# A hybrid encoder on one Trainium2 core: the attention's hand-written step order is replaced by another

## Chip, cores and metric

The kernel runs on one core of one Trainium2 chip. The metric is device microseconds of one execution, as the median of several. The engines are called by the profile's names: PE (TensorE; PEld its weight loads), ACT (ScalarE), DVE (VectorE), POOL (GpSimd) and SP, which here only issues DMAs.

## The reference, cut to what matters

Two layers on x of shape 256 x 1024, float32. Each layer is a half SwiGLU, a mixer and a half SwiGLU; the second layer's mixer is multi-head latent attention, and the change lies in it alone:

```python
cq = rmsnorm(h @ w_dq, q_norm_g)                     # 256 wide
q = (cq @ w_uq).reshape(B, L, 16, 64 + 32)           # rotary part turned with cos, sin
ckv_full = h @ w_dkv                                 # 128 + 32 wide
kv = (rmsnorm(ckv_full[..., :128], kv_norm_g) @ w_ukv).reshape(B, L, 16, 64 + 64)
s = einsum('bqhd,bkhd->bhqk', qn, k_nope) + einsum('bqhr,bkr->bhqk', qr, k_rope)
p = softmax(s * scale); o = einsum('bhqk,bkhd->bqhd', p, v)
x = x + o @ w_o
```

## The kernel before, in words

Every float32 operand of a product is split into a high part (rounded by ACT, `split_hi`, L180) and a low residue (source minus high part, `split_lo`, L184, on DVE or, where a flag says so, on POOL). A product is then three matmuls (`mm3`, L199 to L201): high by high, high by low, low by high. PE runs these triples nearly all the time.

The attention (`mla`, L915) treats 16 heads as 8 pairs p, the two heads of a pair as e = 0, 1, and 256 tokens as two tiles t. Weights come as ten units, each one 1 MB or smaller DMA into one of two `raw` buffers and then split into one of four pairs `wh`, `wl`: units 0 to 3 hold the query, key and value weights of two pairs each, 4 to 7 the output rows, 8 and 9 the gate of the next SwiGLU. In front of it runs the SwiGLU of the same layer, behind it another one, whose first products start when the attention's last steps are issued.

One string, `MLA`, gives the order. Each word is a step, a letter with its arguments, and a table (`do`, L1213) maps it to a function. All this is issued inside `manual_schedule` (L1221): each engine takes up its instructions in exactly the order of the words, and the framework adds the waits that the data and the buffers ask for. The steps that matter here:

- on PE: C compresses x to the latents; c transposes them (after DVE's part of c); q or Q the queries of a pair and K or X its keys (small letter q and K into a bank of the pool `mm`, Q and X into one of `acc`); W the values of two pairs for one token tile; S the scores of a head; T transposes its weights (4 transposes); V the weighted values of a pair; P its part of the output projection; J transposes for the next SwiGLU;
- on ACT and DVE together (high part on ACT, residue on DVE): d for the latents, v for the values, f and h for the keys, H for the turned weights, O for a pair's result; on ACT alone g (queries' high part), E (exponentials, L1143) and w (a piece of a weight unit); on DVE alone a, b, c (normalisation), e (rotary factor on the queries, L1100), M (maxima, L1136 and L1137), N (weigh by 1/sum, L1149 and L1152), F (add to x), x (a weight residue), s (swap rotary columns of the weights, L1049);
- on POOL: y (a weight residue, as x), I (queries' residue), r (as s); on SP: L (load a unit).

So a head goes S, M, E, N, T, H, and its pair V, O, P. The weights of a unit go L, w, x or y.

Two PSUM pools have four banks each of 128x512 float32 (L131, L132). A tile takes a bank at its first write and gives it back when its last reader is done; a later tile that is given this bank waits for those readers, on PE and in PE's order. The values W of pairs 2j, 2j+1 share one tile from the first W of j until v has read both pairs; a T tile lives until its H is done, an S tile until its M and E, a V tile until its O, a K tile until f and h.

```python
self.mm = pool("mm", 4, space=bass.MemoryType.PSUM)        # L131
def turn(p, e):                                             # T
    pr, _ = state[p, e, "p"]
    tr = state[p, e, "t"] = self.bank()
    for k in range(NT):
        for t in range(NT):
            self.transpose(tr[:, k * S + t * P:k * S + (t + 1) * P], pr[:, t * S + k * P:t * S + (k + 1) * P])
def turned(p, e):                                           # H
    state[p, e, "pT"] = self.pl()
    self.split(*state[p, e, "pT"], state[p, e, "t"])
def values(p):                                              # V
    po = state[p, "v"] = self.bank()[:, :S]
```

Of the kernel before, what the change touches and what calls it, by code (L numbers as in the profile page):

```python
# [34 lines left out]
# The order in which the engines take up the steps of the first products, of the mixer and of the attention:  # L35
# the letter of a step (see the tables in first(), mixer() and mla()) and its arguments.
# [43 lines left out]
def shape_constants():  # L80
    """Tables that depend on the shapes alone."""
    f32 = np.float32
    t = np.linspace(0.0, 1.0, S).astype(f32)
    w = (2.0 * math.pi * np.arange(S, dtype=f32) / S).astype(f32)
    f = np.linspace(1e-4, 15.0, 16).astype(f32)
    ph = (w[:, None] * f[None, :]).astype(f32)
    z = np.concatenate([t[:, None], np.cos(ph), -np.sin(ph)], axis=-1).astype(f32)
    c = {"c_zT": z.T, "c_negt": -t.reshape(2, P).T}

    n = np.arange(S, dtype=np.float64)  # L90
    th = 2 * math.pi * (n + 0.5) / (2 * S)
    ang = n[:, None] * th[None, :]
    co, si = np.cos(ang), np.sin(ang)
    rows = lambda m: m.reshape(2, P, S).transpose(1, 0, 2)
    c["c_dft"] = np.stack([rows(co), rows(si), rows(co.T / S), rows(si.T / S)], axis=1).reshape(P, U)

    pos = np.arange(S)
    cnt = [np.clip(pos - v // 2 + v, 0, S) - np.clip(pos - v // 2, 0, S) for v in WINDOWS]
    edge = np.array(WINDOWS)[:, None] / np.stack(cnt)
    c["c_edge"] = np.stack([edge[:, :8], edge[:, -8:]], axis=1).reshape(1, 64)  # L100

    inv = (f32(10000.0) ** (-np.arange(0, ROPE, 2, dtype=f32) / f32(ROPE))).astype(f32)
    ang = (pos.astype(f32)[:, None] * inv[None, :]).astype(f32)
    cos, sin = np.cos(ang).astype(f32), np.sin(ang).astype(f32)
    cc = np.concatenate([cos, cos], axis=1)
    ss = np.concatenate([-sin, sin], axis=1)
    c["c_kr"] = np.concatenate([cc, ss], axis=1).reshape(2, P, 64).transpose(1, 0, 2)
    one = np.ones((64, S))
    c["c_q"] = np.stack([np.concatenate([one, cc.T, ss.T]), np.concatenate([cc.T, ss.T, one])], axis=1)
    return {k: np.ascontiguousarray(v, dtype=f32) for k, v in c.items()}  # L110
# [9 lines left out]
class Net:  # L120
# [32 lines left out]
    def load_unit(self, parts, ncols, step=1024, lo_pool=False, post=None, rows=P, queue=None):  # L153
        """Starts the transfers of a unit; returns its tiles and the steps that split it."""
# [37 lines left out]
    def rows(self, w, k0, nk, c0, nc_):  # L192
        """Rows (k0..k0+nk)*128 of w, columns c0.. as [128, nk, nc_]."""
        return w[k0 * P:(k0 + nk) * P, c0:c0 + nc_].rearrange("(k p) c -> p k c", p=P)

    def mm3(self, out, xh, xl, wh, wl, start, stop):
        """out += x.T @ w with x stationary."""
        t = self.nc.tensor
# [11 lines left out]
    def spread(self, out, cols):  # L210
        """Each column [128, 1] as a row on all partitions: out[:, j*128..] = cols[j].T"""
# [5 lines left out]
    def square(self, x, half):  # L217
        """The part of mean(x^2) of a half of x's columns, per partition."""
# [5 lines left out]
    def rstd(self, sums):  # L224
        """1/sqrt(mean(x^2) + eps) per partition."""
# [7 lines left out]
    def prep(self, x, t, half, g, xT):  # L233
        """Columns t*128.. of the half of xT (hi, lo) = (x * g).T"""
# [41 lines left out]
    def spin(self, n):  # L276
        """Products of zeros, which bring the tensor engine to its full clock before there is data."""
# [37 lines left out]
    def ffn(self, r, xT, late, wg, wu, wd, finish, hooks=(), early=None, mid=None, pre=None, tail=False):  # L315
# [96 lines left out]
        def first():  # L412
            """The first products, in the order in which x and the weights arrive."""
# [7 lines left out]
            def load_w(u, c, n):  # L421
                """Rows c.. of unit u: 0, 1 of the gate, 2, 3 of the other factor, 4, 5 of the next chunk's gate."""
# [81 lines left out]
    def filter_steps(self, hy, fl):  # L504
        """The steps that make self.spec[o][kc] = [re | im] of the normalised filters, bias in the real part."""
# [153 lines left out]
    def mixer(self, hy, mx, cur, nxt, wg, pre, hold, dump=None):  # L659
# [52 lines left out]
        def scaled(ct):  # L712
            """The projection times r, with a margin of zeros."""
# [13 lines left out]
        def spread_r():  # L727
            """r of every token along the free axis, on all partitions."""
# [24 lines left out]
        def turn(cc):  # L753
            """Channel tiles cc (even), cc + 1 in turn into a bank [time, (t, 256 channels)]."""
            j = cc % 2
            if not j:
# [14 lines left out]
        z, Y = [None, None], [[None, None], [None, None]]  # L771

        def spectrum(half, kc):
            """The spectrum of the half at the frequencies of kc, [k, re | im]"""
# [55 lines left out]
        def pool_sums(g):  # L830
            u = state["u", g]
            # after the loop b[i] holds the sum over i-w/2 .. i+w/2-1
# [82 lines left out]
    def mla(self, ml, cur, nxt, wg, pre, hold, dump=None):  # L915
        """A generator: it yields where the work of the block before goes on."""
# [12 lines left out]
        # chunks 0, 1: queries' latent; 2: keys' and values' latent; 3: rotary key, four times  # L929
# [3 lines left out]
        # values: [token tile, head, 128 channels], the channels of the other head zero  # L933
# [25 lines left out]
        def moments(t, *parts):  # L959
            """The factors of the latents' normalisation: part 0 of the keys' and values', 1 of the queries'."""  # L960
            ps, em = latent[t], small("em", 1)
            # r * (r^2 ss / n + eps)^-1/2 = (ss / n + eps / r^2)^-1/2
# [65 lines left out]
        def queries_view(m):  # L1028
            """Queries [pair, k, head, 128] of a unit of weights."""
            return m[:, :C_KV].rearrange("p (n k e c) -> p n k e c", n=2, k=2, e=2)  # L1030

        def load(u):
            """Units 0..3: weights of the pairs 2u, 2u+1; 4..7: their output rows; 8, 9: of the next block's gate."""
# [10 lines left out]
        def rotated(u, part, engine=nc.vector):  # L1044
            """The columns of the rotary channels once more, their halves swapped."""
# [5 lines left out]
        def piece(u, c):  # L1051
            """Both parts and the weights of piece c. Of two pairs' weights: 0 the even heads' queries, 1 and 3 the odd
            heads' plain and rotary ones, 2 the keys and values."""
# [16 lines left out]
        def queries(p, pool=None):  # L1070
            """Queries of pair p from the latents."""
# [18 lines left out]
        def pair_values(j, t):  # L1090
            """Values of the pairs 2j, 2j+1 at the tokens t."""
            if not t:
# [142 lines left out]
def encoder(ctx, tc, a, out, upto=99, dbg=None):  # L1235
# [5 lines left out]
    def then(i, j):  # L1241
        """What follows an update of x[t]: the next block's input."""
# [38 lines left out]
    def last(t, half):  # L1281
        """Half of the result's rows t: x * gain right away, the rest once both halves are there."""
# [96 lines left out]
```

## Time and profile before

| what | value |
|---|---|
| median of the runs | 983.23 us (two of the three runs: 982.95 and 983.23) |
| profiled execution | span 981.6 us, mean granted clock of PE 0.996 |
| first compression of the attention (C0.1) to the end of its last projection | 698.4 to 788.4 us of the span |

The profiled execution has no time of its own besides its span; what lies around the span is the 1.6 us by which the median is larger. A line number in a row (L204) is that of the kernel before; many steps share the lines of a helper, so a row is recognised by its tile names (`mm<-ident,h` are the transposes T, `ph<-mm` and `pl<-mm` the two halves of H, `oh<-mm` and `ol<-mm` those of O, `acc<-wh,oh` the projections P).

### The profile page before, as it was taken

The page shows a single profiled execution, that of the slowest core. Times are in us where ns is not written, and L with a number is a line of the kernel's source. Part 1 is how long each engine was busy: PE and PEld are TensorE (multiplying, and loading weights), DVE is VectorE, ACT ScalarE, POOL GpSimd, SP SyncE. Part 2 cuts the span into 40 slices and gives each one's busy share as a digit, 9 for nine tenths or more (in the row PEclk, how much of TensorE's full clock was granted, in tenths as well). Part 3 has the DMA queues.
Part 4 walks back from the last instruction along what each step waited for, and adds up shares of the span by engine and source line. Part 5 has one row for each costly group of instructions (what it writes and reads, how often), then busy time and mean ns, then how long its engine had stood idle before and what let it go on. Part 6 is the DMA issues. An engine that isn't in the chain of part 4 may idle for free.

```text
span 981.6 us, 12399 instructions
## 1 busy us (share of the span) xinstructions
PE 959.8 (98%) x4816; PEld 805.5 (82%) x4816; DVE 613.7 (63%) x820; ACT 492.5 (50%) x773; POOL 176.0 (18%) x223
## 2 busy tenths in 40 slices
PE   8999999999999999999999999999989999999997
PEld 6878888879998788888888888888788878888885
DVE  5576576768887754544575454445898875454454
ACT  5546456445545554344454454344677764434442
POOL 1300013445877200000000000000364410000000
PEclk9999999999999999999999999999999999999999
DMA  7765655615324665565537645564232266556641
GB/s 258 241 223 189 209 172 172 215 43 156 116 86 151 215 214 187 179 212 193 172 122 224 212 172 192 182 215 151 88 101 86 87 218 232 176 178 211 207 129 43
DMA packets 80539, 167.56 MB, mean 171 GB/s; under 512 B 3660, under 2 KB 24005, under 8 KB 80160
## 3 DMA queue, kind: packets, MB, share of 16 engines
q1 hardware_dynamic: 79152, 164.27, 51.0%
q0 software_dynamic: 1040, 1.98, 0.7%
q8 instruction: 38, 0.62, 0.3%
q10 hardware_dynamic: 288, 0.52, 0.1%
q14 instruction: 21, 0.17, 0.1%
HBM read 165.18 MB, written 1.05 MB: 169 GB/s over the span
## 4 chain that ended last, share of the span: by engine, by line
PE 82%; DVE 9%; DMA 3%; ACT 3%; issue 2%; POOL 1%; SPq 0%; POOLq 0%; ACTq 0%; DVEq 0%
PE mm L201 16%; PE mm L200 16%; PE mm L199 16%; PE acc L199 9%; PE acc L201 9%; PE acc L200 9%; PE mm L204 3%; DVE wl L184 2%; DMA raw<-mix_w_in 1%; DVE h L1152 1%; DVE pl L184 1%; ACT wh L180 1%; DMA x<-x 1%; DMA raw<-ffn_w_down 1%; DMA raw<-ffn_w_up 1%
## 5 line engine op out<-in xcount | busy, mean ns | idle before, releaser
L184 DVE TENSOR_TENSOR wl<-raw,wh 128x1024 fp32r<-128x1024 f32 (+3 forms) x310 | 346.2, 1148 | 264.7 <-ACT wh L180 264.4
L180 ACT ACTIVATE wh<-raw 128x1024 fp32r<-128x1024 f32 (+2 forms) x370 | 318.9, 904 | 278.9 <-PE mm L201 110.7
L199 PE MATMUL mm<-wh,xTh 128*128 128x512 f32 x704 | 276.9, 393 | 0.0
L201 PE MATMUL mm<-wh,xTl 128*128 128x512 f32 x704 | 274.8, 390 | 0.0
L200 PE MATMUL mm<-wl,xTh 128*128 128x512 f32 x704 | 274.3, 390 | 0.0
L201 PEld LDWEIGHTS mm<-wh,xTl 128*128 128x128 f32 x704 | 132.1, 188 | 28.4 <-DVE xTl L184 0.6
L200 PEld LDWEIGHTS mm<-wl,xTh 128*128 128x128 f32 x704 | 132.3, 188 | 27.2 <-DVE wl L184 0.5
L199 PEld LDWEIGHTS mm<-wh,xTh 128*128 128x128 f32 x704 | 132.2, 188 | 26.9 <-issue 0.4
L199 PE MATMUL acc<-wh,ph 128*128 128x512 f32 x352 | 139.9, 397 | 0.0
L200 PE MATMUL acc<-wl,ph 128*128 128x512 f32 x352 | 137.8, 392 | 0.0
L201 PE MATMUL acc<-wh,pl 128*128 128x512 f32 x352 | 137.6, 391 | 0.0
L207 POOL TENSOR_TENSOR r<-ms,mhalf 128x1 f32<-128x1 f32 x14 | 10.7, 763 | 569.7 <-DVE ms L228 569.7
L184 POOL TENSOR_TENSOR wl<-raw,wh 128x512 fp32r<-128x512 f32 (+3 forms) x60 | 77.2, 1303 | 47.1 <-ACT wh L180 43.3
L199 PEld LDWEIGHTS acc<-wh,ph 128*128 128x128 f32 x352 | 66.1, 188 | 13.9 <-issue 1.1
L201 PEld LDWEIGHTS acc<-wh,pl 128*128 128x128 f32 x352 | 66.1, 188 | 13.7
L200 PEld LDWEIGHTS acc<-wl,ph 128*128 128x128 f32 x352 | 66.2, 188 | 12.7
L354 ACT ACTIVATE s<-mm,r 128x512 f32<-128x512 f32 (+1 forms) x48 | 31.2, 652 | 56.9 <-PE mm L201 56.0
L356 DVE SCALAR_TENSOR_TENSOR h<-mm,r,s 128x512 f32<-128x512 f32 (+1 forms) x48 | 33.7, 703 | 28.4 <-PE mm L201 23.6
L184 DVE TENSOR_TENSOR pl<-mm,ph 128x512 fp32r<-128x512 f32 (+1 forms) x66 | 42.7, 651 | 13.1 <-ACT ph L180 12.8
L180 ACT ACTIVATE ph<-mm 128x512 fp32r<-128x512 f32 (+1 forms) x66 | 37.0, 563 | 25.0 <-PE mm L204 24.8
L204 PE MATMUL mm<-ident,h 128*128 128x128 f32 x240 | 36.7, 273 | 3.2 <-ACT oh L180 1.3
L204 PEld LDWEIGHTS mm<-ident,h 128*128 128x128 f32 x240 | 29.4, 140 | 11.0 <-DVE h L1152 1.7
(315 smaller groups left out, 1122.8 us busy)
## 6 DMA issues: line engine op xcount, KB each, us to landing
raw<-ffn_w_down SPq DMA_DIRECT2D x44, 1024.0 KB, 5.0
raw<-ffn_w_up SPq DMA_DIRECT2D x39, 1024.0 KB, 5.1
raw<-ffn_w_gate SPq DMA_DIRECT2D x38, 1024.0 KB, 5.1
raw<-mix_w_in SPq DMA_DIRECT2D x8, 1024.0 KB, 5.6
raw<-ffn_w_gate SPq DMA_DIRECT2D x8, 512.0 KB, 3.9
raw<-ffn_w_up SPq DMA_DIRECT2D x8, 512.0 KB, 4.9
raw<-mix_w_out SPq DMA_DIRECT2D x4, 1024.0 KB, 4.9
raw<-mla_w_o SPq DMA_DIRECT2D x4, 1024.0 KB, 5.0
```

The lines of the kernel that those rows point to most:

```text
L180: return self.nc.scalar.activation(hi, src, AF.Copy)
L184: return eng.tensor_tensor(out=lo, in0=src, in1=hi.bitcast(F32), op=ALU.subtract)
L199: t.matmul(out=out, lhsT=xh, rhs=wh, start=start, stop=False)
L200: t.matmul(out=out, lhsT=xh, rhs=wl, start=False, stop=False)
L201: t.matmul(out=out, lhsT=xl, rhs=wh, start=False, stop=stop)
L204: self.nc.tensor.transpose(out=out, in_=in_, identity=self.ident)
L207: self.r_ins = self.nc.gpsimd.tensor_tensor(out=out, in0=in_, in1=self.mhalf[:, :1].to_broadcast(list(in_.shape)), op=ALU.pow)
L354: nc.scalar.activation(s[:, :w], ps_g, AF.Silu, scale=r[t])
L356: nc.vector.scalar_tensor_tensor(out=hh[:, :w], in0=ps_u, scalar=r[t], in1=s[:, :w], op0=ALU.mult, op1=ALU.mult)
L1152: nc.vector.tensor_scalar(out=pr[:, c], in0=pr[:, c], scalar1=rc[:, t:t + 1], scalar2=None, op0=ALU.mult)
```

## The change

The string is replaced by another of the same 337 words but for eight. Five words of DVE go to POOL (s1.1 becomes r1.1; x2.3, x7.3, x8.1, x9.0 and x9.2 become y2.3, y7.3, y8.1, y9.0 and y9.2, which makes six with s1.1) and two of POOL go to DVE (y8.3 and y9.1 become x8.3 and x9.1). Everything else is order. Of the table only the lines around the places below are shown:

```diff
-    "w4.0 E0.0 f3 e3 e2 w4.1 S1.0 r3.0 Q4 w4.3 N0.1 Q5 M1.0 N0.0 E1.0 g3 M1.1 y3.1 I3 T0.0 T0.1 e5 h3 H0.0 v2 N1.0 Q6 "
-    "Q7 H0.1 y3.2 g5 S3.0 w4.2 M3.0 g2 E1.1 L5 N1.1 E3.0 X4 e6 V0 T1.0 I5 k2 S3.1 y4.0 T1.1 I2 O0 P0.1.0 y4.3 e4 S2.0 "
...
+    "X4 M0.0 S1.0 w4.3 E0.1 y3.0 e2 w3.1 f3 M1.0 Q5 e5 h3 S1.1 E0.0 I3 W3.1 M1.1 r3.1 y3.1 N0.0 E1.0 N0.1 L5 N1.0 "
+    "S3.0 M3.0 y4.3 E1.1 w4.2 T0.0 H0.0 g2 Q4 k2 W2.1 v2 e4 f4 T0.1 I2 r3.0 y4.2 H0.1 T1.0 H1.0 S2.0 M2.0 y4.1 V0 "
+    "E3.0 N1.1 w5.3 O0 S3.1 S2.1 M3.1 E2.0 P0.0.0 T1.1 M2.1 N3.0 g5 K5 N2.0 L6 Q6 E3.1 H1.1 Q7 E2.1 V1 N3.1 T3.0 f5 "
+    "g4 T3.1 N2.1 I4 e6 P0.0.1 O1 H3.0 W2.0 P1.0.1 H3.1 h5 e7 P1.0.0 y5.3 w5.0 w5.2 y5.2 I5 T2.0 V3 w6.0 h4 v5 y5.0 "
...
         def pair_values(j, t):
-            if not t:
+            if ("v", j) not in state:
                 state["v", j] = self.bank()
```

The second hunk lets the token tiles of W come in either order; the mixer's transposes get the same rule, without an instruction moving. Comments and docstrings go, and the new string has one line more, so that a line number in the changed kernel is one higher (L205 for L204). In the SwiGLU behind the attention two instructions move with it: on ACT the loading of the Silu table and the first Silu stand ahead of the splits of the second `up` unit, where they stood behind them, and on DVE half a weight residue stands ahead of the second product with the Silu.

PE, the transposes and the scores between V0 and P of pair 0. In the rows, `mm` is a bank's tile with its number, `h` a head's weights, `kt0h`, `kt2h` the keys of the pairs 0 or 3 and 2, `ph` the queries; the names in brackets are the engines waited for. Before, T1.0, S3.1 and T1.1:

```order
L204 MATMUL mm_6296<-ident_82,h_6177 128x128 [waits PE_49]
L204 MATMUL mm_6296<-ident_82,h_6177 128x128 x3
L199 MATMUL mm_6306<-kt0h_5676,ph_6181 128x256 [waits Activation_49]
L200 MATMUL mm_6306<-kt0l_5677,ph_6181 128x256
L201 MATMUL mm_6306<-kt0h_5676,pl_6182 128x256
L199 MATMUL mm_6306<-kt0h_5676,ph_6181 128x256
L200 MATMUL mm_6306<-kt0l_5677,ph_6181 128x256
L201 MATMUL mm_6306<-kt0h_5676,pl_6182 128x256
L204 MATMUL mm_6314<-ident_82,h_6261 128x128 [waits DVE_49,Activation_49]
L204 MATMUL mm_6314<-ident_82,h_6261 128x128 [waits DVE_49]
L204 MATMUL mm_6314<-ident_82,h_6261 128x128 x2
```

The same engine with the change: W2.1, T0.1, T1.0 and the head of S2.0, one right behind the other.

```order
L200 MATMUL mm_6241<-wh_5836,lath_5674 128x256 [waits DVE_49]
L201 MATMUL mm_6241<-wl_5837,lath_5674 128x256
L202 MATMUL mm_6241<-wh_5836,latl_5675 128x256
L205 MATMUL mm_6251<-ident_82,h_6124 128x128 [waits DVE_49]
L205 MATMUL mm_6251<-ident_82,h_6124 128x128 x3
L205 MATMUL mm_6264<-ident_82,h_6180 128x128 [waits DVE_49]
L205 MATMUL mm_6264<-ident_82,h_6180 128x128 x3
L200 MATMUL mm_6273<-kt2h_5680,ph_6221 128x256 [waits DMAHW0_49,DVE_49]
L201 MATMUL mm_6273<-kt2l_5681,ph_6221 128x256 [waits DMAHW1_49]
L202 MATMUL mm_6273<-kt2h_5680,pl_6222 128x256 [waits Pool_49]
```

T1.0 stood behind V0 and waited for nothing of DVE; now T0.1, T1.0 and S2.0 follow each other, and each waits for DVE.

PE again, a little later: the transposes of pair 3 (T3.0, T3.1). Before, with the projection P1.0.0 between them:

```order
L204 MATMUL mm_6442<-ident_82,h_6273 128x128 [waits DVE_49,Activation_49]
L204 MATMUL mm_6442<-ident_82,h_6273 128x128 x3
L199 MATMUL acc_6383<-wh_6068,oh_6374 128x512
L200 MATMUL acc_6383<-wl_6069,oh_6374 128x512
L201 MATMUL acc_6383<-wh_6068,ol_6375 128x512
L204 MATMUL mm_6461<-ident_82,h_6423 128x128 [waits DVE_49,Activation_49]
L204 MATMUL mm_6461<-ident_82,h_6423 128x128 [waits DVE_49]
L204 MATMUL mm_6461<-ident_82,h_6423 128x128 x2
```

With the change, from the end of V1 (`mm_6400`) to P0.0.1:

```order
L1175 MATMUL mm_6400<-pl_6380,v1h_5686 128x256
L1176 MATMUL mm_6400<-ph_6379,v1l_5688 128x256
L205 MATMUL mm_6417<-ident_82,h_6297 128x128 [waits DVE_49]
L205 MATMUL mm_6417<-ident_82,h_6297 128x128 x3
L205 MATMUL mm_6427<-ident_82,h_6375 128x128 [waits DVE_49]
L205 MATMUL mm_6427<-ident_82,h_6375 128x128 x3
L200 MATMUL acc_6439<-wh_5950,oh_6306 128x512
L201 MATMUL acc_6439<-wl_5951,oh_6306 128x512 [waits Pool_49]
L202 MATMUL acc_6439<-wh_5950,ol_6307 128x512
```

V1, T3.0 and T3.1 now stand side by side, and the projections come after them.

DVE, the end of the latents (`latl` are their residues in d, `wl<-wl` the swap s1.1, `wl<-raw,wh` the residue x2.3). Before:

```order
L184 TENSOR_TENSOR latl<-acc,lath 128x4x128
L993 SCALAR_TENSOR_TENSOR h<-acc,rq,gb 128x256
L184 TENSOR_TENSOR latl<-acc,lath 128x2x128
L1049 COPY wl<-wl 128x4x2x16 x2
L184 TENSOR_TENSOR wl<-raw,wh 128x4x32
L184 TENSOR_TENSOR latl<-acc,lath 128x2x128
L1013 CAST kt0l<-latl 64x256 x2
```

And with the change:

```order
L185 TENSOR_TENSOR latl<-acc,lath 128x4x128
L994 SCALAR_TENSOR_TENSOR h<-acc,rq,gb 128x256
L185 TENSOR_TENSOR latl<-acc,lath 128x2x128 x2
L1014 CAST kt0l<-latl 64x256 x2
L1101 TENSOR_TENSOR s<-mm,cqt 128x512
```

The swap and the residue no longer stand between the two last residues of the latents.

## Rows read from the trace of the kernel before

**Rows 1.** The page: busy time of each engine, share of the span, instructions.
```profile
PE 959.8 (98%) x4816; PEld 805.5 (82%) x4816; DVE 613.7 (63%) x820; ACT 492.5 (50%) x773; POOL 176.0 (18%) x223
```

**Rows 2.** Busy time by stretch (PE, PEld, DVE, ACT, POOL; then granted PE clock).
```profile
698.40:788.40 90.00, 83.23 (x557) 75.35 (x556) 80.97 (x181) 64.20 (x178) 47.86 (x50) 0.98 0.28 91
...
735.00:736.00 1.00, 0.98 (x2) 0.82 (x3) 1.00 (x3) 1.00 (x3) 0.00 (x0) 0.50 0.08 16
```

**Rows 3.** Waits of PE from 690 to 800 us: total, times, longest.
```profile
PE acc L204 <- DVE h L993: 1.6, 1, 1.6
PE mm L204 <- ACT oh L180: 1.3, 1, 1.3
PE mm L204 <- DVE h L1152: 1.2, 2, 0.9
PE mm L1173 <- DVE pl L184: 1.1, 2, 0.9
PE mm L204 <- DVE ol L184: 0.7, 1, 0.7
PE mm L1079 <- DVE latl L184: 0.7, 1, 0.7
PE mm L204 <- DVE x L1195: 0.5, 1, 0.5
```

**Rows 4.** DVE in order of time: s1.1.
```profile
709.38 1.44 DVE L1049 CAST wl<-wl 128x128 fp32r<-128x128 f32 x2
```

**Rows 5.** In order of time: T7.1 on PE, H7.1 on ACT and DVE.
```profile
777.58 0.60 PE L204 MATMUL mm<-ident,h 128*128 128x128 f32 x4
...
778.28 0.60 ACT L180 ACTIVATE ph<-mm 128x512 fp32r<-128x512 f32 x1
...
778.91 0.69 DVE L184 TENSOR_TENSOR pl<-mm,ph 128x512 fp32r<-128x512 f32 x1 [0.45 <-ACT ph L180]
```

**Rows 6.** The chain: PE's pace (transposes, matmuls of 256 and 512); ACT's exponentials.
```profile
777.75 0.44 PE mm L204 x4
...
712.59 0.12 PE mm L1079
...
752.10 0.23 PE acc L200
...
739.97 0.91 ACT h L1143 x4
```

**Rows 7.** In order of time: V7's last matmul on PE, then O7.
```profile
780.78 0.28 PE L1175 MATMUL mm<-ph,v3l 128*128 128x256 f32 x1
...
781.16 0.39 ACT L180 ACTIVATE oh<-mm 128x256 fp32r<-128x256 f32 x1 [1.12 <-PE mm L1175]
...
781.57 0.42 DVE L184 TENSOR_TENSOR ol<-mm,oh 128x256 fp32r<-128x256 f32 x1 [0.48 <-ACT oh L180]
```

**Rows 8.** DVE in order of time: M1.0, then one N.
```profile
722.49 0.68 DVE L1136 TENSOR_REDUCE mx<-mm 128x2 f32<-128x512 f32 x1
723.20 0.17 DVE L1137 TENSOR_SCALAR mx<-mx 128x2 f32<-128x2 f32 x1
723.28 0.16 DVE L1149 RECIPROCAL rc<-sm 128x2 f32<-128x2 f32 x1
723.47 0.61 DVE L1152 TENSOR_SCALAR h<-h,rc 128x256 f32<-128x256 f32 x2
```

**Rows 9.** DVE in order of time: e5, then h3.
```profile
724.80 0.69 DVE L1100 TENSOR_TENSOR s<-acc,cqt 128x512 f32<-128x512 f32 x1
725.41 0.85 DVE L184 TENSOR_TENSOR kt0l<-acc,kt0h 64x256 fp32r<-64x256 f32 x2
```

**Rows 10.** DVE and POOL in order of time: N1.1; y4.3, y4.1.
```profile
731.76 2.52 DVE L1152 TENSOR_SCALAR h<-h,rc 128x256 f32<-128x256 f32 x2
...
731.59 2.54 POOL L184 TENSOR_TENSOR wl<-raw,wh 128x512 fp32r<-128x512 f32 x2
```

**Rows 11.** Groups by shape, DVE, 700 to 800 us: N, busy us, mean ns.
```profile
L1152 DVE TENSOR_SCALAR h<-h,rc 128x256 f32<-128x256 f32 x32 | 17.2, 578 | 0.6
```

More of the change, by code (lines that the diff above doesn't have):

```diff
@@ L755, in turn @@
             j = cc % 2
-            if not j:
+            if ("T", cc // 2) not in state:
                 state["T", cc // 2] = self.bank()
```

23 rows, old and new, of the table MLA are left out of this document.

## The prediction

> **What bounds the kernel now.** I read the page first. PE is busy for 959.8 us, 98% of the span [rows 1]. Whatever another order can give must therefore lie in PE's missing 2%, and whatever it can cost appears as a new wait of PE, since a product that comes late has no idle stretch behind it to be caught up in. Next I read the busy times by stretch. The attention takes 90.0 us, from 698.4 to 788.4, of which PE is busy for 83.2 [rows 2]: 6.8 us idle. The mean granted clock of the stretch is 0.98, which is 90.0 x 0.02 = 1.8 us lost, at one place: the stretch from 735 to 736 runs at 0.50, the lower of the two levels, 1.2 GHz [rows 2]. So 8.6 us of the attention are not PE's work; 81.4 are. The list of PE's waits names them [rows 3]: 1.6 for the normalised latents (c1.0), 0.7 for their last residue (q0), 1.3 and 0.9 at T1.1 (the second and the longest of the third row), and in the next rows the pieces of V3, V5, T3.1 and T5.1, 0.2 to 0.9 each; 0.5 falls behind the attention, where a transpose waits for x. The clock is low in the projection just behind T1.1: in the stretch ahead of it PE had two waits with one transpose between them.
>
> The other engine to watch is DVE, busy for 81.0 of the 90.0 [rows 2]. ACT has 64.2, POOL 47.9.
>
> **The change part by part.** The profiled execution has no time beside its span of 981.6; the median is 983.2, so 1.6 lie around the span and I add differences to the median.
>
> First, what stays. PE's work is the same instructions, 81.4 us. c1.0's wait of 1.6 stays: on DVE the same steps stand ahead of it.
>
> Second, what goes. Before q0 DVE had s1.1, 1.44 [rows 4], and x2.3 between the latents' last two residues; both leave for POOL, so q0's 0.7 goes [rows 3]. Of this I give back 0.3 at S0.1, the first scores, which now come before a second pair's keys and wait for DVE's h0. POOL has room for the two: it is busy for half the stretch, and its first consumer, Q3, comes several products later. T1.1's two waits and the clock loss behind them (1.3 + 0.9 + 1.8) belong to a place that exists no more, as do the four small ones. The 0.5 at x goes too: F1.1 is now followed by more of PE's own work. So of 8.6 only 1.6 is carried over, and 0.3 new.
>
> Third, what comes: PSUM banks. The pool `mm` has four. With the change W3.1 is issued before T0.0, and its tile lives until v7, near the end; W2.1 follows behind Q4, and its tile lives until v4, behind V3. Before, W2 came after S2.1 and W3 after the projections of pair 4, so that three banks went round. Now two do from Q4 to T2.1, and three from there, where before there were three or four. At T0.1 one of the two holds S3.0 until E3.0, which on ACT stands behind H1.0. So T0.1, T1.0 and S2.0 must use the same bank one after the other; the order shows it, each now waits for DVE. The price of each such pair is read from cycles that the trace shows without a queue in them:
> - T, then its H: T7.1 starts at 777.58, H's residue ends at 779.60 [rows 5]. PE's own part is 0.44 [rows 6], so the next user of that bank waits 2.02 - 0.44 = 1.6. Four places: T0.1 to T1.0, T1.0 to S2.0, T1.1 to K5, T3.0 to T3.1: 6.4. A fifth, T5.1 to V4, has S7.0 between (six matmuls of 0.12, 0.7, [rows 6]): 0.85.
> - V, then its O: V7's last matmul starts at 780.78 and the next one could 0.12 later; O's residue ends at 781.99 [rows 7]: 1.1. Two places, V0 to S3.1 and V1 to T3.0: 2.2.
> - S, then M and E: 0.16 until the result is there (a matmul lasts 0.28 [rows 7] and the next starts after 0.12 [rows 6]), M 0.8 [rows 8], E 0.91 [rows 6]: 1.9. S3.1 to T1.1 has S2.1 (0.7) and one projection (three matmuls of 0.23, 0.7, [rows 6]) between: 0.5. S5.1 to V2 has K7 (0.36) and a projection: 0.85. S4.1 to S4.0 has more, but E4.1 stands on ACT behind H2.1, which waits for the T2.1 just ahead of S4.0: 0.16 + 0.60 [rows 5] + 0.91 = 1.7.
>
> That is 12.5, forced by neighbours on PE: only if PE came late by itself would they be less, and PE has nothing else that makes it late.
>
> Fourth, queues on DVE. T0.0 takes S1.1's bank; M1.1 stands behind e5 (0.6) and the residues h3 (0.86) [rows 9] and is followed by E1.1: from S1.1 on 0.16 + 0.6 + 0.86 + 0.8 + 0.91 = 3.3 against W3.1, S3.0 and S1.1 itself (0.36 + 0.72 + 0.72): 1.5. W2.1 takes T0.0's bank; H0.0's residue stands behind three N and M3.0 (3 x 0.76 + 0.8 = 3.1, [rows 8]) and lasts 0.69, of which E1.1, T0.0 and Q4 cover 0.91 + 0.44 + 1.44: 1.0. T4.0 waits for f7 and h7 behind O2: 0.5. Sum 3.0. These are estimates out of rows with no contention in them; their bounds are 0 (DVE came early) and 6 (twice as much).
>
> The residues that move in the last third (x7.3 and a net one of units 8 and 9, 0.7 each on DVE, 1.27 on POOL, [rows 10]) I set at nothing: PE is fed there by projections, and the gate's second unit is needed only 2.7 us into the gate's products. If that cover went, x9.1 or y9.3 would cost about 1. L9 is issued later, since its `raw` buffer waits for y7.0; w9.0 stands on ACT behind O7 and comes later still. Behind the attention the Silu table and the first Silu stand ahead of the second `up` unit's splits: nothing, as the gate's products are some 11 us long.
>
> Sum: 12.5 + 3.0 + 1.6 + 0.3 = 17.4 against 8.6, and the 0.5 behind: +8.3. **983.2 + 8.3 = 991.5 us.** At the low end the forced waits are a fifth shorter (hand-overs that overlap) and the queues cost nothing: 10.0 + 1.9 - 8.6 - 0.5 = +2.8, 986. At the high end the queues cost 6, and the next rival's 3 and one more clock loss of 1.8 come on top: +16, 999.
>
> A rule that speaks against moving residues: N1.1 took 2.52 just while POOL did two residues in 2.54 [rows 10], where N0.0 took 0.61 [rows 8]. All 16 N took 17.2 us [rows 11], undisturbed they would make 16 x 0.61 = 9.8: 7.4 us of DVE are paid for POOL's residues already. By these rows each residue given to POOL saves DVE 0.7 and can cost it 1.27. The Trainium skill says the same (SBUF — State Buffer, Who interferes with whom): VectorE's two-port modes and GpSimd share a port pair under an exclusive lock, and the loser blocks for the whole instruction. The trace agrees here. In the new order POOL is out of work just when N0.0 to N1.0 run (its next step, I2, waits for g2 behind H0.0 on ACT), so the sum has it at nothing.
>
> **The rivals.**
> - *The lock decides.* If POOL's steps do meet M and N on the chains above (M3.0 against I2, M4 and M5 against I5 and y5.0), three of them are late by a residue of 1.27, some 3 to 4: 995. For it: rows 10. Against: POOL has only two or three residues of 512 columns more than before, and most of them late.
> - *The clock stays down.* Between T0.0 and T3.1 PE would do about 14 us of work with ten of the waits between. Before, two waits of 1.3 and 0.9 with a transpose between were enough for 0.50. If half of this stretch, or all of it, runs at 0.50, 7 to 14 us come on top: 998 to 1005. Against: a single wait of 1.6 at c1.0 did not do it, and the projections and queries fill the array in between. The Trainium skill describes such a case (TensorE: Matmul & The Clock Gate, A second HAM failure mode: psum-queue depth-cycling): short idles between groups of matmuls that cycle through PSUM banks make the clock swing between its levels; rows 2 and 3 show one such swing, after the densest waits.
> - *The bank waits aren't there (not slower).* The order names the engine waited for, not the step. If T1.0 and T3.1 wait for their own N, long done, and not for the H of the transpose ahead, then the 12.5 fall away, and what is left is 4.9 against 8.6 and 0.5: -4.2, 979. It decides at T0.1: T1.0 follows within 0.5 us, or after 2. For it: three banks went round before without such a wait on PE. Against: the lifetimes, counted above.
> - That the change doesn't do what it says is excluded: the order shows the steps moved.
>
> **How the numbers follow.** Forecast 991.5 with its own range of 986 to 997: 0.63. The lock, 995 to 999: 0.10. The clock: 0.11, of which 0.04 above 1002.9, the 2% above which a measurement of this kernel can tell a change. No bank waits, 976 to 984: 0.16, hardly any of it 2% faster, since PE's work alone is 981.6 - 8.6 - 0.5. The range of 984 to 999 leaves out most of the last case and the worse part of the clock's. Faster 0.01, same 0.95, slower 0.04.
>
> **What would show it.** In the changed kernel's trace: the attention about 98 us long with PE still busy for some 81; among PE's waits transposes and scores behind `pl`, the residue of H, with 1.4 to 1.6 each, and behind `ol` with about 1; T0.1 and T1.0 some 2 us apart; no wait at the first queries. Wrong if the transposes stand side by side without a wait, if PE idles for less than 9 us in the attention, or if the largest loss is a granted clock of 0.50 over ten microseconds or more.

## The result, and the profile after

| | before | after |
|---|---|---|
| median | 983.54 us | 998.25 us (997.52 to 999.41, four runs) |
| ratio, 95% interval | | 1.0150, 1.0138 to 1.0163 |
| profiled execution, span | 981.6 us | 997.6 us (its time 999.41) |
| attention, first compression to last projection or transpose | 698.4 to 788.4: 90.0 | 698.0 to 805.5: 107.5 |
| behind it, to the end of the span | 193.2 | 192.1 |

(One of the four runs of before took 1195.07; it is not in the ratio, and without it the median of before is 983.23.) The changed kernel is 14.7 us slower, where 8.3 were forecast. In the two profiled executions the spans differ by 16.0: the attention is 17.5 longer, what follows is 1.1 shorter, and it starts 0.4 earlier. The profiled execution is the longest of the four, with a mean granted clock of 0.989; the other three had 0.991 and 0.992.

The page's line of busy times, which answers to [rows 1]:

```profile
PE 968.2 (97%) x4816; PEld 812.7 (81%) x4816; DVE 606.3 (61%) x815; ACT 492.8 (49%) x773; POOL 179.2 (18%) x228
```

PE has the same 4816 matmuls and is busy for 8.4 us longer. So not all of the loss is idle time. The busy times by stretch, with the columns of [rows 2]: the whole attention, then the three stretches in it at the lower clock level. Before, the one such stretch is 3.4 us long, around the place in [rows 2].

```profile
698.00:805.50 107.50, 90.61 (x558) 80.77 (x557) 73.90 (x177) 64.86 (x178) 49.23 (x54) 0.92 0.25 80
709.70:713.10 3.40, 3.40 (x19) 3.40 (x18) 2.32 (x3) 2.94 (x8) 3.40 (x7) 0.50 0.09 21
733.60:743.80 10.20, 8.56 (x35) 7.83 (x36) 4.80 (x14) 4.20 (x15) 0.00 (x0) 0.50 0.31 103
754.10:757.50 3.40, 3.40 (x12) 2.83 (x11) 2.22 (x5) 2.54 (x5) 1.18 (x1) 0.50 0.00 0
```

PE idles for 107.5 - 90.6 = 16.9 us, against 6.8 before, and is busy for 90.6, against 83.2, mostly because 17.0 us run at a granted clock of 0.50, against 3.4 before. The first of the three stretches follows c1.0's wait, the second the transposes T0.0 to T1.0, the third T3.0 and T3.1.

PE's waits in the attention, the columns as in [rows 3]; L205 are the transposes, L200 and L201 here scores and values, L1174 weighted values, L1087 keys:

```profile
PE mm L205 <- DVE pl L185: 3.5, 3, 1.5
PE acc L205 <- DVE h L994: 2.0, 1, 2.0
PE mm L200 <- DVE pl L185: 1.8, 2, 1.5
PE mm L200 <- ACT h L1144: 1.7, 1, 1.7
PE mm L205 <- ACT h L1144: 1.6, 1, 1.6
PE mm L1087 <- DVE pl L185: 1.5, 1, 1.5
PE mm L1174 <- ACT h L1144: 1.0, 1, 1.0
PE mm L200 <- DVE ol L185: 0.9, 1, 0.9
PE mm L205 <- DVE ol L185: 0.9, 1, 0.9
PE mm L1174 <- DVE pl L185: 0.8, 1, 0.8
PE mm L205 <- DVE kt1l L185: 0.6, 1, 0.6
PE mm L1174 <- DVE ol L185: 0.2, 1, 0.2
PE mm L201 <- DVE kt0l L185: 0.2, 1, 0.2
```

These are sixteen waits of 16.7 us. Before, `pl` held PE up for 1.1 in all [rows 3]; now it does for 3.5 + 1.8 + 1.5 + 0.8 = 7.6. By steps: T1.0, S2.0, K5 and T3.1 wait 1.47 each for the residue of the transpose ahead of them; S3.1 and T3.0 0.93 each for a pair's result; S4.0 1.66, T0.0 1.64 and V2 1.05 for exponentials whose scores held the bank; V4 0.76, T4.0 0.60, T5.0 0.57, W2.1 0.36, V5 0.22, S0.1 0.16; and c1.0 1.97. The wait at the first queries (q0) is gone.

One hand-over, in order of time: T0.1 on PE, the two halves of H0.1, T1.0, the two halves of H1.0, the first score of S2.0 (start, duration, engine; in brackets the idle time and what ended it):

```profile
730.11 0.60 PE L205 MATMUL mm<-ident,h 128*128 128x128 f32 x4
...
730.80 0.60 ACT L181 ACTIVATE ph<-mm 128x512 fp32r<-128x512 f32 x1 [0.87 <-PE mm L205]
731.43 0.69 DVE L185 TENSOR_TENSOR pl<-mm,ph 128x512 fp32r<-128x512 f32 x1 [0.92 <-ACT ph L181]
732.18 0.65 PE L205 MATMUL mm<-ident,h 128*128 128x128 f32 x4 [1.47 <-DVE pl L185]
732.93 0.60 ACT L181 ACTIVATE ph<-mm 128x512 fp32r<-128x512 f32 x1 [1.53 <-PE mm L205]
...
733.56 0.69 DVE L185 TENSOR_TENSOR pl<-mm,ph 128x512 fp32r<-128x512 f32 x1 [1.44 <-ACT ph L181]
...
734.31 0.58 PE L200 MATMUL mm<-kt2h,ph 128*128 128x256 f32 x1 [1.47 <-DVE pl L185]
```

ACT and DVE take up the tile one after the other, and PE idles until both are done. T1.0 starts 2.07 after T0.1 instead of the 0.44 of PE's pace [rows 6]: 1.63 are lost, of which the list of waits shows 1.47. The other 0.16 fits the time until a first matmul behind a wait is through: a matmul's 0.28 [rows 7] less the pace of 0.12 [rows 6]. The list counts it as busy.

### The profile page after: what moved, and what is told of

Same layout as the page of the kernel before. It is cut to its first block, busy times and chain, and to the rows that moved or that the text cites. A ratio compares the mean times of both kernels' runs of the same rounds, so it can differ in the third digit from the quotient of the medians.

```text
span 997.6 us, 12403 instructions
## 1 busy us (share of the span) xinstructions
PE 968.2 (97%) x4816; PEld 812.7 (81%) x4816; DVE 606.3 (61%) x815; ACT 492.8 (49%) x773; POOL 179.2 (18%) x228
## 3 DMA queue, kind: packets, MB, share of 16 engines
HBM read 165.18 MB, written 1.05 MB: 167 GB/s over the span
## 4 chain that ended last, share of the span: by engine, by line
PE 84%; DVE 7%; issue 2%; ACT 2%; DMA 2%; POOL 1%; SPq 0%; POOLq 0%; ACTq 0%; DVEq 0%
PE mm L200 16%; PE mm L201 16%; PE mm L202 16%; PE acc L200 9%; PE acc L202 9%; PE acc L201 9%; PE mm L205 4%; DVE wl L185 2%; DVE pl L185 1%; ACT ph L181 1%; ACT wh L181 1%; DMA raw<-mix_w_in 1%; PE mm L1174 0%; DMA raw<-ffn_w_down 0%; DMA raw<-ffn_w_up 0%
## 5 line engine op out<-in xcount | busy, mean ns | idle before, releaser
L181 ACT ACTIVATE wh<-raw 128x1024 fp32r<-128x1024 f32 (+3 forms) x370 | 318.9, 903 | 273.8 <-PE mm L202 115.8
L200 PE MATMUL mm<-wh,xTh 128*128 128x512 f32 x704 | 277.2, 394 | 0.0
L201 PE MATMUL mm<-wl,xTh 128*128 128x512 f32 x704 | 274.5, 390 | 0.0
L200 PEld LDWEIGHTS mm<-wh,xTh 128*128 128x128 f32 x704 | 132.4, 188 | 27.1 <-issue 0.4
L201 PEld LDWEIGHTS mm<-wl,xTh 128*128 128x128 f32 x704 | 132.4, 188 | 26.8
L200 PE MATMUL acc<-wh,ph 128*128 128x512 f32 x352 | 140.0, 398 | 0.0
L201 PE MATMUL acc<-wl,ph 128*128 128x512 f32 x352 | 137.8, 391 | 0.0
L185 POOL TENSOR_TENSOR wl<-raw,wh 128x512 fp32r<-128x512 f32 (+3 forms) x63 | 80.1, 1285 | 38.6 <-ACT wh L181 35.3
L200 PEld LDWEIGHTS acc<-wh,ph 128*128 128x128 f32 x352 | 66.1, 188 | 13.8 <-issue 1.1
L201 PEld LDWEIGHTS acc<-wl,ph 128*128 128x128 f32 x352 | 66.2, 188 | 12.7
L205 PE MATMUL mm<-ident,h 128*128 128x128 f32 x240 | 37.2, 275 | 6.7 <-DVE pl L185 3.5
L205 PEld LDWEIGHTS mm<-ident,h 128*128 128x128 f32 x240 | 29.6, 141 | 15.1 <-DVE pl L185 3.4
```

The lines of the kernel that those rows point to most:

```text
L181: return self.nc.scalar.activation(hi, src, AF.Copy)
L185: return eng.tensor_tensor(out=lo, in0=src, in1=hi.bitcast(F32), op=ALU.subtract)
L200: t.matmul(out=out, lhsT=xh, rhs=wh, start=start, stop=False)
L201: t.matmul(out=out, lhsT=xh, rhs=wl, start=False, stop=False)
L205: self.nc.tensor.transpose(out=out, in_=in_, identity=self.ident)
```

## The experiments

Theory: the value tiles of W3.1 and W2.1, written early and read late, take two of the four banks, and the steps that then follow each other on one bank wait for ACT and DVE; the low clock is a consequence of PE's idle time. Rivals: the rest of the new order makes the loss; the residues on POOL do; the clock falls for another reason. Every run was timed in rounds with the kernel before on one chip, whose median there was 984.2 to 984.7; the ratios are to that (the quotient of two medians differs from them by up to 0.0007).

### Both W steps put back

```diff
-E0.0 I3 W3.1 M1.1
+E0.0 I3 M1.1
...
-Q4 k2 W2.1 v2
+Q4 k2 v2
...
-H3.0 W2.0 P1.0.1
+H3.0 W2.0 W2.1 P1.0.1
...
-N7.0 W3.0 w7.1
+N7.0 W3.0 W3.1 w7.1
```

> The changed order with W3.1 put back beside W3.0 and W2.1 beside W2.0, all else as in the changed order. Banks theory (the loss comes from two value tiles that hold two of four banks from early on, and the low clock is a consequence of the waits): the same-bank neighbours get different banks, so PE idles for 6 to 8 us in the attention instead of 16.9, at most 3.5 us run at a granted clock of 0.50 instead of 17, time 984 to 988. Rival (the order of the other steps, and the residues on POOL, make the loss; banks only name it): idle stays above 13 and the time at 995 or more.

Measured: 980.38 us, ratio 0.9950 (0.9934 to 0.9967). Two words moved give back all of the loss, and 4 us more. The attention by stretch, and its two low stretches; then PE's waits:

```profile
701.20:789.90 88.70, 83.53 (x558) 77.25 (x557) 74.70 (x177) 64.14 (x178) 49.30 (x54) 0.96 0.30 97
...
711.30:714.70 3.40, 3.40 (x18) 3.23 (x17) 2.52 (x6) 1.57 (x4) 3.40 (x7) 0.50 0.47 180
735.20:738.60 3.40, 3.40 (x17) 3.40 (x17) 2.14 (x7) 1.81 (x8) 0.55 (x1) 0.50 0.51 122
```

```profile
PE acc L205 <- DVE h L994: 2.0, 1, 2.0
PE mm L205 <- DVE pl L185: 1.5, 1, 1.5
PE mm L205 <- DVE h L1153: 1.1, 1, 1.1
PE mm L201 <- DVE kt0l L185: 0.5, 2, 0.3
PE mm L1174 <- DVE pl L185: 0.2, 1, 0.2
```

Of the sixteen waits c1.0, T0.0, T1.0 and a few small ones are left, 5.2 us in all, and nothing behind V0 waits any more. The bank theory stands and the rest of the new order is cleared: it is better than the old one. More was won than I expected. The clock part was missed the other way, 6.8 us at 0.50 instead of 3.5 or less. But that is one execution: the profiled one took 983.86 at a mean granted clock of 0.992, the other three 979.66 to 980.50 at 0.996 and 0.997.

### One W step put back

```diff
-E0.0 I3 W3.1 M1.1
+E0.0 I3 M1.1
...
-N7.0 W3.0 w7.1
+N7.0 W3.0 W3.1 w7.1
```

> The changed order with W3.1 alone put back beside W3.0; W2.1 stays early, so three banks go round from Q4 to T2.1. Banks theory: about half of the waits of T1.0, S2.0, K5 and T3.1 go (those whose neighbour then has another bank), idle of PE 9 to 13 us, time 988 to 993. If W3.1 alone were the culprit: 984 to 988, as with both put back. Rival of the other steps: 995 or more.

Measured: 983.14 us, ratio 0.9981 (0.9968 to 0.9994); PE's waits in the attention are 6.8 us. The other step alone, W2.1 from behind Q4 to behind W2.0:

> The changed order with W2.1 alone put back beside W2.0; W3.1 stays early, so three banks go round. Banks theory: with W3.1 alone put back 18 of the 20 us were won, because one bank more for the pair T0.1 to T3.1 was enough; W2.1 alone gives a bank back for the same stretch, but W3.1's tile lasts until v7, so the places behind T2.1 (S4.0, V2, T4.0, T5.0, V4) stay as they are: 984 to 990. If W3.1 were the culprit by itself: 993 or more.

Measured: 987.59 us, ratio 1.0034 (1.0021 to 1.0046); waits 10.7. As expected the waits behind T2.1 are those of the changed kernel (S4.0 1.66, V2 1.04, T4.0 0.61, T5.0 0.56, V4 0.76) and those between T0.0 and T2.1 fall from 8.1 to 2.1; one low stretch of 3.4 is left. The first run beat its expectation: of the changed kernel's 2.0% against the better order, W3.1 alone gives 1.7 and W2.1 alone 1.2 (the second expectation had 18 of 20 us for W3.1; it is 17 of 20). So the price is not so much per bank: two banks going round are too few, and three nearly do.

### One W step moved early in the order of before

```diff
-Q7 H0.1 y3.2 g5 S3.0
+Q7 H0.1 y3.2 g5 W3.0 S3.0
...
-N7.0 W3.0 W3.1 E7.1
+N7.0 W3.1 E7.1
```

> The order of before with one word moved: W3.0 (whose tile then lives until v7) stands ahead of S3.0 instead of beside W3.1. Banks theory: one bank less from S3.0 on makes new neighbours on one bank, V1 to S2.1 (1.1), T3.0 to T3.1 (1.6 less a projection of 0.7) and S3.1 behind V0 with T1.0 between (1.1 less 0.44), 2.7 together, and some of the clock: 2 to 7 us slower than before. Theory that the loss belongs to the rest of the new order: within 1 us of before.

Measured: 991.89 us, ratio 1.0074 (1.0059 to 1.0089), 7.3 us slower, just above what was expected. Its attention and PE's longest waits:

```profile
698.80:796.20 97.40, 85.53 (x558) 75.69 (x557) 82.79 (x181) 64.72 (x178) 47.58 (x50) 0.98 0.26 84
```

```profile
PE mm L205 <- DVE pl L185: 2.4, 2, 1.3
...
PE mm L205 <- DVE ol L185: 1.5, 1, 1.5
PE mm L200 <- ACT h L1144: 1.4, 2, 0.8
PE mm L200 <- DVE ol L185: 1.3, 2, 0.9
PE mm L200 <- DVE kt0l L185: 1.1, 1, 1.1
```

One word in the old order makes half of the loss, so an early W tile costs time in either order. S2.1 behind V1 waits 0.94 and T3.1 behind T3.0 1.28, the neighbours named; others appear that I had not counted (T2.0 and S5.1 1.15 each, among them). There is one low stretch of 3.4, as long as before's: here the loss is not the clock's. PE idles for 5.1 us more than before, and is busy for 2.3 more, of which 0.16 behind each of five more waits makes 0.8.

### The residues back on their engines

```diff
-W0.1 y2.3 K1
+W0.1 x2.3 K1
...
-W1.1 r1.1 h2
+W1.1 s1.1 h2
...
-E7.1 y7.1 y7.3 P5.0.1
+E7.1 y7.1 x7.3 P5.0.1
...
```

(and in the same way y8.1, y9.0 and y9.2 to DVE, x8.3 and x9.1 to POOL)

> The changed order with the eight residue steps back on the engine that they had before (six on DVE, two on POOL), each at its new place in the order. Banks theory: PE's waits behind the transposes stay, the time within 996 to 1002 (q0 waits for DVE again, 0.5 to 2 more). Residues theory (what POOL got delays M, N and the chains): at least 4 us faster than the changed kernel, 994 or less.

Measured: 1000.61 us, ratio 1.0157 (1.0142 to 1.0172), no better than the changed kernel's 1.0150. PE's waits behind the transposes stand there with the same lengths. The same edit on the run with both W steps put back:

> The order of the run with both W steps put back, with the eight residue steps on the engine that they had before. It shows what of the 4 us by which that run beats the kernel before belongs to the residues. If the residues on POOL bring it: 983 or more. If it is the order of the other steps: 980 to 982 (s1.1 ahead of h2 and x2.3 ahead of k0 delay DVE by 0.7 to 1.4 at a place where PE has one bank to spare).

Measured: 980.45 us, ratio 0.9960 (0.9945 to 0.9975), not to be told apart from 0.9950. The eight residues change nothing that can be measured in either order; the gain of the new order lies in its other steps.

### Products that nobody reads, in the waits

```diff
+        def fill(n):
+            ps, w = self.bank(self.acc), self.ones.bitcast(BF16)
+            for _ in range(n):
+                nc.tensor.matmul(out=ps[:, :S], lhsT=w[:, :P], rhs=w[:, :S], start=True, stop=True)
...
-w4.2 T0.0 H0.0
+w4.2 Z12 T0.0 H0.0
...
-H0.1 T1.0 H1.0 S2.0
+H0.1 Z11 T1.0 H1.0 Z11 S2.0
...
```

(Z is a fill of n products; c1.0 gets Z15, K5 and T3.1 Z11, S3.1 and T3.0 Z6.)

> The changed order with extra bfloat16 products of constants, whose result nobody reads, on PE ahead of eight steps that wait (15 ahead of c1.0, 12 ahead of T0.0, 11 ahead of T1.0, S2.0, K5 and T3.1, 6 ahead of S3.1 and T3.0; 83 matmuls of 256 columns, some 9 us of PE work inside the waits). Waits stay forced by ACT and DVE, so nothing is saved but the clock. Theory that the low clock follows from PE's idle time: the time at a granted clock of 0.50 falls from 17 us to under 4, and the time by 5 to 7, to 991 to 993. Theory that the clock falls for another reason, or that the projections behind the waits would have waited anyway: 997 to 1000.

Measured: 995.86 us, ratio 1.0109 (1.0094 to 1.0124): 0.41% or 4.0 us faster than the changed kernel, where 5 to 7 were expected. In the profiled executions the attention is 5.7 shorter:

```profile
699.90:801.70 101.80, 93.16 (x641) 82.15 (x640) 74.07 (x177) 64.69 (x178) 49.19 (x54) 1.00 0.26 85
```

```profile
PE mm L200 <- ACT h L1144: 1.9, 2, 1.7
PE mm L205 <- DVE pl L185: 1.1, 3, 0.6
...
PE mm L205 <- ACT h L1144: 0.7, 1, 0.7
```

The eight waits stand there, now filled but for at most 0.4 each, and the granted clock is 1.00 through the whole attention: no stretch at 0.50 is left. The mean clock of all four runs is 0.996 to 0.999, against 0.989 to 0.992. So the low clock followed from PE's idle time, and it is worth 4 to 6 us of the loss. One of the filled waits is c1.0, which has nothing to do with the banks: the stretch behind it, 3.4 us long, cost 1.7 of the 7.7 us of PE's work. Not all of the lost clock comes back as time, since a slow PE had covered other waits: T1.1, which did not wait in the changed kernel, now waits 0.68 for E (the row with 0.7).

The same cure for the better order, in its three waits:

> The order of the run with both W steps put back, with extra products that nobody reads on PE inside its three waits (15 ahead of c1.0, 8 ahead of T0.0, 11 ahead of T1.0). It ran at a granted clock of 0.50 for two stretches, together 6.8 us, behind c1.0 and behind T1.0. If the low clock follows from PE's idle time, both go, and the time falls by 1.5 to 3, to 977.5 to 979; if it falls for another reason, no change, 980 to 981, or 1 more for products that come late.

Measured: 979.20 us, ratio 0.9956 (0.9941 to 0.9972). The profiled attention is 2.3 shorter than without the fills, and the clock is up:

```profile
697.30:783.70 86.40, 84.64 (x592) 77.76 (x592) 75.31 (x177) 64.06 (x178) 49.31 (x54) 1.00 0.31 100
```

But the execution without the fills was the longest of its four and this one the shortest of its ten. The ratios, 0.9956 against 0.9950, don't show the gain; whether the fills help there stays open. It is 4 to 5 us faster than the kernel before either way.

### The lost banks kept, the neighbours moved apart

```diff
-T0.1 I2 r3.0 y4.2 H0.1 T1.0 H1.0 S2.0
+T0.1 r3.0 I2 y4.2 H0.1 Q6 T1.0 H1.0 Q7 S2.0
...
-K5 N2.0 L6 Q6 E3.1 H1.1 Q7 E2.1 V1
+K5 N2.0 L6 E3.1 H1.1 E2.1 V1
```

(On POOL, r3.0 and I2 change places too.)

> The changed order with both W steps left early, so that two banks still go round, but with the queries Q6 (into a bank of the other pool) between T0.1 and T1.0, and Q7 between T1.0 and S2.0, instead of behind K5. If the price is that of neighbours on one bank, each query (1.63 us in the trace) covers a hand-over of 1.47, T1.0's and S2.0's waits go (2.9), V1, which loses its cover, waits 0.5 to 1 for E2.1, and the stretch at a granted clock of 0.50 behind them shrinks: 3 to 6 us faster than the changed kernel, 992 to 995. If the lost bank is what costs, wherever the neighbours stand: PE meets the same waits later, 997 or more.

Measured: 994.79 us, ratio 1.0099 (1.0080 to 1.0118), 5.0 us faster than the changed kernel. Of PE's waits two rows answer to those above:

```profile
PE mm L205 <- ACT h L1144: 2.3, 2, 1.6
PE mm L205 <- DVE pl L185: 2.0, 2, 1.5
```

T1.0's and S2.0's 1.47 are gone (`pl` at L205 falls from three waits to two and S2.0's is not there), T1.1 waits 0.69 more (the second in the first row), and the low stretches are 10.2 us together instead of 17.0. V1's new wait, which I expected, did not come. So with two banks the price hangs on which steps stand side by side: a product into a bank of the other pool between them hid a hand-over here.

## Why the prediction was right and wrong

**Mechanism and place: right.** The two early W tiles were named as the cause, and the runs that put them back, both or one, and the one that moves W3.0 in the old order show it. The rival without bank waits is refuted by its own test: T1.0 follows T0.1 after 2.07 us, not 0.5.

**Bank waits: right in size.** Forecast against what PE lost (wait plus 0.16): a transpose behind another's H 1.6 against 1.63, four times; a score or transpose behind O 1.1 against 1.09, twice; S4.0 1.7 against 1.82; V4 0.85 against 0.92; V2 0.85 against 1.21. S3.1 to T1.1 (0.5) did not show while PE ran at half clock there; with the fills it is 0.68.

**DVE queues: right in sum.** Listed, T0.0 waits 1.64 (1.5), W2.1 0.36 (1.0), T4.0 0.60 (0.5); T5.0's 0.57 and V5's 0.22 were not foreseen. c1.0 did not stay at 1.6: it waits 1.97, in all runs of the new order without fills, and no run shows why. q0 went, and S0.1 got 0.16 where the sum had 0.3. The sixteen waits of 16.7 us with 0.16 each behind them make 19.3. Of that 1.3 lay in the 81.4 already, since the kernel before had eight waits in the attention: 18.0, where the sum had 17.4.

**The clock: the term that failed.** The sum carried only c1.0 over from the old 8.6, struck out the old clock loss of 1.8 with its place, and set the new one at nothing; what a fall would cost stood in a rival alone, with a chance of 0.11. PE then spent 17.0 us at 0.50, in 15.4 of which it was busy (3.40, 8.56 and 3.40 in the rows of the section on the result): 7.7 us of its work are lost there. The forecast made the attention 81.4 + 17.4 = 98.8. Measured are 16.9 of idle time and, without what the clock took, 90.6 - 7.7 = 82.9 of work: 99.8, only 1.0 more. The 7.7 make it the measured 107.5. Without the low clock the attention is not 7.7 but 5.7 shorter, as the run with the fills shows, since other waits come out.

The argument that misled me was that c1.0's wait of 1.6 had no fall behind it and that projections and queries lie between the others. But the first of the three stretches now lies behind c1.0 itself, and from T0.0 to S2.0 PE meets 1.64, 0.36, 1.47 and 1.47 within nine microseconds, more than twice the idle time ahead of the place in [rows 2, 3] where the clock had already fallen. The rival's 998 to 1005 begins where the time came out. The rule that I cited for it, in the Trainium skill (TensorE: Matmul & The Clock Gate, A second HAM failure mode: psum-queue depth-cycling), is borne out by the run with the fills: the banks and hand-overs are the same, PE idles for 8.6 us instead of 16.9, and the granted clock is 1.00.

**The lock: the other way.** The N group, which answers to [rows 11]:

```profile
L1153 DVE TENSOR_SCALAR h<-h,rc 128x256 f32<-128x256 f32 x32 | 12.0, 418 | 0.6
```

The sixteen N took 12.0 us instead of 17.2. POOL's 49.2 us of work lie in 107.5 us instead of 47.9 in 90.0, which fits with the two engines meeting less. It is not the moved residues that do it: with the eight back on their engines the N take 12.0 as well. That DVE's 5.2 us bought nothing is argued and not shown: the hand-overs PE waits for are one ACT and one DVE step in a row, each at the length that the sum had for it. Setting the moved residues at nothing was right: both runs that move them back show no difference.

**The range and the signs.** 998.25 lies inside 984 to 999, near its upper end, and outside the forecast's own 986 to 997. "Same", a change of less than 2%, was given 0.95, and that came true. Of the signs, T0.1 and T1.0 some 2 us apart, the lengths behind `pl` and `ol` and no wait at the first queries are there; the attention of about 98 us with PE busy for some 81 is not: it is 107.5, with 90.6. Of the signs of being wrong the last is half met: 17.0 us ran at 0.50, but the waits are the larger loss. That the time still lies in the range is partly luck: its upper end added 3.0 for the queues, 3 for the lock and 1.8 for the clock to the sum, and what came was little of the first, nothing shown of the second, and 7.7 of PE's work for the third.

## What to carry to other kernels

Before a step is issued earlier, count how long the buffer lives that it takes: a tile written early and read late takes its bank out of the rotation, and the price appears at steps that were not touched. With only two banks going round, count the neighbours on PE: each pair that shares a bank costs the whole way over ACT and DVE, unless a product into another bank stands between. And where such waits come closely, price the clock too: a few unread products in the waits are a cheap test of how much of a loss is clock.

## What had not been expected of the hardware

The granted clock does not follow from one wait, nor from the order of the steps. Behind the same wait of 1.97 at c1.0 it fell to 0.50 in the changed kernel (709.70 to 713.10) and with both W steps put back (711.30 to 714.70), but not with the residues put back, though all steps up to c1.0 are the same; the 6 us behind it read there:

```profile
709.00:715.00 6.00, 5.90 (x47) 5.60 (x48) 5.28 (x11) 4.82 (x12) 5.45 (x8) 1.00 0.57 185
```

In the order of before it did not fall behind c1.0's wait of 1.62; with W3.0 moved, a word that comes long after c1.0, it fell behind 1.61:

```profile
709.90:713.30 3.40, 3.40 (x18) 3.40 (x17) 3.18 (x7) 1.71 (x5) 2.99 (x6) 0.50 0.41 90
```

Executions of one kernel differ as well: the ten with W3.1 alone put back had mean clocks of 0.993 to 0.999, and took 983.44 and 985.16 at 0.993, 980.78 and 979.65 at 0.999. What decides it these runs do not show. A profile shows one execution; another of the same kernel can have more or fewer microseconds at 0.50.

A low clock can also hide a wait: T1.1 had none in the changed kernel and 0.7 as soon as the clock was up (0.67 also with the residues put back, where its place ran at 1.00). That is part of why 7.7 us of lost PE work came back as only 5.7.
